# Two transposes of a hybrid attention trunk move from TensorE to VectorE and to the stores

## The chip, the cores and the metric

The kernel runs on one core of a Trainium2 chip. The metric is device time in microseconds for one launch. The core has five engines, each with an instruction queue of its own that is worked in order: TensorE (PE: matrix products, and transposes as products with an identity), VectorE (DVE), ScalarE (ACT), GpSimd (POOL) and SyncE (SP), which here does nothing but issue DMAs. Sixteen DMA engines carry the transfers that SP and ACT issue.

## The reference

One layer of a hybrid trunk over 2048 latent tokens behind 256 context tokens, width 1024. One projection of the normalized input feeds two token mixers; the one that matters here is a gated DeltaNet with four heads of 128, run forward and backward over chunks of 64 tokens. Cut to what the change touches:

```python
def _gdn_inputs(qkv_raw, ...):
    qkv = silu(_short_conv(qkv_raw, conv_w))          # 5 taps along the tokens
    q, k, v = split(qkv)                              # 4 heads of 128 each
    q, k = _l2norm(q) * 128 ** -0.5, _l2norm(k)

def _gdn_chunked(q, k, v, g, beta, s0, ...):          # for each direction
    gc = cumsum(g)                                    # within a chunk of 64 tokens
    decay = where(incl, exp(gc[:, None] - gc[None, :]), 0)
    a_mat = where(strict, (kb @ kc.T) * decay, 0)     # the keys' decayed Gram matrix
    t_mat = triangular_solve(a_mat, eye)              # its inverse, unit lower triangular
    u, w = t_mat @ (vc * bc), t_mat @ (kb * exp(gc))
    ...                                               # scan over the chunks with u, w, q, k
```

Everything is float32 in and out; the large products are split into high and low float32r parts.

## The kernel before

Eighteen blocks of 128 tokens (two of context, sixteen of latent) are worked in this order. First come the input norms, the transposed input `hh`/`hl` and the attention keys. Then `qkv(ORDER)` runs over the column blocks m of the projection: the four value heads m = 8 to 11, then the four key heads m = 4 to 7, and after them the four query heads m = 0 to 3 together with the attention queries. For each m there are five segments (256 tokens of context, four times 512 latent tokens): `fm_dense` on PE gives `lps` with channels on the partitions, ScalarE copies it to `y`, `conv` makes `cacc` (four passes on VectorE at L625, one more at L627 with ScalarE's tanh ahead of it), and `finish` does what the head needs. So there are twenty calls of `finish` for the value heads and twenty for the key heads, each on nn = 2 or 4 blocks.

For a value head, `finish` needs the tokens on the partitions: PE transposes each 128x128 block of `cacc` into the PSUM tile `zt` (L657), ScalarE copies it to `st` (L675), and one DMA stores it to `vsp` (L648).

For a key head, `finish` also stores `cacc` itself (`kTsp`, L654), makes the transposed keys the same way (`ksp`), and forms the Gram matrix of each block: `gps` on PE (L666), times the decay tile `dtl`, which is loaded from `Dsp` (L632) into a single buffer, gives `p` on VectorE (L668). `p` serves the backward direction. Its transpose serves the forward direction: PE transposes (L680) into the same two PSUM buffers as `gps`, ScalarE copies to `pt` (L682). Of each of the two, `spill_blocks` stores the two 64x64 diagonal squares to `Nsp` (L639, two DMAs) and one 64x64 off-diagonal square to `offsp` (L640, one DMA). `p` and `pt` share the tag `o` of two buffers.

Later, `base` loads the planes of `Nsp` with one 64x64 square on each partition (L796) and inverts them on VectorE, beside the gate projections (`rest_run`) on PE; `base4` does the same for the last four blocks (L839), and the scan loads `vsp`, `ksp` and `offsp`.

The order of each engine's instructions is fixed when the program is built: a planner simulates the program and lays every queue out in the order of its simulated times. In the run an engine waits at the head of its queue for the semaphores that the instruction names. Nothing behind it passes.

Of the kernel before, what the change touches and what calls it, by code (L numbers as in the profile page):

```python
# [7 lines left out]
F32 = mybir.dt.float32  # L8
# [11 lines left out]
NC = NB + NCB  # L20
H = 4
# [19 lines left out]
def _hybrid(ctx, tc, nc, V, S, G, T, ins, out, dbg, upto):  # L41
    dma = nc.sync.dma_start
# [5 lines left out]
    def dscr(name, shape, dt=F32):  # L48
        return dram.tile(shape, dt, name=name)
# [10 lines left out]
    ident = cst.tile([128, 128], F32, name="ident")  # L60
# [21 lines left out]
    g = pers.tile([128, NC, 8], F32, name="g")  # L82
# [9 lines left out]
    ksp = dscr("ksp", [NC, 128, H, 128])  # L92
    vsp = dscr("vsp", [NC, 128, H, 128])
    Dsp = dscr("Dsp", [NC, 128, H, 128])

    Nsp = [dscr(f"Nsp{d}", [NC, H, 2, 64, 64]) for d in range(2)]
    offsp = [dscr(f"offsp{d}", [NC, 64, H, 64]) for d in range(2)]
    QDsp = dscr("QDsp", [NB, 128, H, 128])
    brT = dscr("brT", [NC, 8, 128])
# [43 lines left out]
    def psum(tag, shape, dt=F32, name=None):  # L143
        _, p, banks = pst["left" if tag in pst["left"][2] else "right"]
        return p.tile(shape, dt, name=name or tag, tag=tag, bufs=banks[tag])
# [104 lines left out]
    if True:  # L250
# [283 lines left out]
        for gi in range(8):  # L534
# [10 lines left out]
            o = gi % 2 * 256  # L545
# [89 lines left out]
    def spill_blocks(d, t, c0, nn, h):  # L635

        for b in range(2):
            r = slice(b * 64, b * 64 + 64)
            dma(Nsp[d][c0:c0 + nn, h, b].rearrange("c r i -> r c i"), t[r, :, r])  # L639
        dma(offsp[d][c0:c0 + nn, :, h].rearrange("c r i -> r c i"), t[64:128, :, 0:64])  # L640

    def finish(m, z, c0, n):

        h = m % 4
        nn = n // 128
        b0 = c0 - NCB
        zc = [z[:, j * 128:(j + 1) * 128] for j in range(nn)]
        spill = lambda dst, t: dma(dst.rearrange("c p d -> p c d"), t)  # L648
        if m < 4:
            dma(qTsp[h, :, b0 * 128:b0 * 128 + n], z)  # L650
            kT = pb.tile([128, 4, 128], F32, name="kTl", tag="st")
            dma(kT, kTsp[h, :, c0 * 128:c0 * 128 + n].rearrange("p (c t) -> p c t", t=128))
        elif m < 8:
            dma(kTsp[h, :, c0 * 128:c0 * 128 + n], z)  # L654
        ps = psum("zt", [128, 4, 128])
        for j in range(nn):
            T.transpose(ps[:, j], zc[j], ident)  # L657
        if m < 8:
            dt = decay_of(h, c0, nn)
            for j in range(nn):  # L660
                junk = pb.tile([128, 128], BF16, name="junk", bufs=1)
                dst = ssk[:, c0 + j, h:h + 1] if m >= 4 else alpha[:, b0 + j, h:h + 1]
                S.activation(junk, ps[:, j], AF.Square, accum_out=dst)
            gps = psum("gps", [128, 4, 128])
            for j in range(nn):
                T.matmul(gps[:, j], lhsT=zc[j] if m >= 4 else kT[:, j], rhs=zc[j], start=True, stop=True)  # L666
            p = pb.tile([128, 4, 128], F32, name="p", tag="o")[:, :nn]
            V.tensor_tensor(p, gps[:, :nn], dt, op=ALU.mult)  # L668
            if m >= 4:
                spill_blocks(1, p, c0, nn, h)  # L670
            else:
                spill(QDsp[b0:b0 + nn][:, :, h], p)
        if m >= 4:
            st = pb.tile([128, 4, 128], F32, name="st")[:, :nn]
            S.copy(st, ps[:, :nn])  # L675
            spill((ksp if m < 8 else vsp)[c0:c0 + nn, :, h], st)
        if 4 <= m < 8:
            pps = psum("gps", [128, 4, 128])
            for j in range(nn):
                T.transpose(pps[:, j], p[:, j], ident)  # L680
            pt = pb.tile([128, 4, 128], F32, name="pt", tag="o")[:, :nn]
            S.copy(pt, pps[:, :nn])  # L682
            spill_blocks(0, pt, c0, nn, h)

    def qkv(order, after, w=None, beside=()):
        w = w or weights(w_in[:, order[0] * 128:order[0] * 128 + 128], KT)
# [95 lines left out]
    def base(si, npool, pool, fr, bk):  # L782


        n = 8 * len(fr)
        h1 = max(32, n)
        N = npool.tile([128, 64, 64], F32, name="N")
        nb = npool.tile([128, 64], F32, name="nb")
        if n < h1:
            G.memset(N[0:h1], 0.0)  # L790
            G.memset(nb[0:h1], 0.0)
        for d, chunks in ((0, fr), (1, bk)):
            for i0, c, k in runs(chunks):
                p0 = d * h1 + i0 * 8
                dma(nb[p0:p0 + 8 * k], brT[c:c + k, d * 4:d * 4 + 4].rearrange("c h (b t) -> c (h b) t", b=2))
                dma(N[p0:p0 + 8 * k], Nsp[d][c:c + k].rearrange("c h b r i -> (c h b) r i"))  # L796
        for q in range(4):
            r, w = slice(q * 16, q * 16 + 16), q * 16 + 16
            V.tensor_tensor(N[0:h1, r, 0:w], N[0:h1, r, 0:w],
                            nb[0:h1, 0:w].unsqueeze(1).to_broadcast([h1, 16, w]), op=ALU.mult)  # L800
            V.tensor_tensor(N[h1:h1 + n, r, 0:w], N[h1:h1 + n, r, 0:w],
                            nb[h1:h1 + n, r].unsqueeze(2).to_broadcast([n, 16, w]), op=ALU.mult)
        yield 9
        A = N[0:h1 + n]
        for m in range(1, 63):
            tmp = pool.tile([128, 1376], F32, name="btmp")
            r = 63 - m
            tv = tmp[0:h1 + n, :r * m].rearrange("p (r j) -> p r j", j=m)
            V.tensor_tensor(tv, A[:, m + 1:, m].unsqueeze(2).to_broadcast([h1 + n, r, m]),  # L809
                            A[:, m, 0:m].unsqueeze(1).to_broadcast([h1 + n, r, m]), op=ALU.mult)  # L810
            V.tensor_tensor(A[:, m + 1:, 0:m], A[:, m + 1:, 0:m], tv, op=ALU.add)  # L811
            yield 2 * (65 + 1.04 * r * m) / 1e3

        for q in range(4):
            r, w = slice(q * 16, q * 16 + 16), 64 - q * 16
            G.affine_select(A[:, r, q * 16:], A[:, r, q * 16:], pattern=[[1, 16], [-1, w]], base=0,
                            channel_multiplier=0, compare_op=ALU.is_gt, fill=0.0)
        V.memset(A.rearrange("p r c -> p (r c)")[:, ::65], 1.0)
        for d, chunks in ((0, fr), (1, bk)):
            p0 = d * h1  # L820
            dma(Xset[d][si].rearrange("c h b r j -> (c h b) (r j)"), N[p0:p0 + n].rearrange("p r j -> p (r j)"))
            for ci, c in enumerate(chunks):
                Xsp[d][c] = Xset[d][si][ci]
        yield 1

    def base4(fr, bk):


        N = bs2.tile([128, 64, 64], F32, name="N")
        nb = bs2.tile([128, 64], F32, name="nb")  # L830
        buf = bs2.tile([128, 1376], F32, name="btmp")
        X = buf[:, 0:1024].rearrange("p (r s) -> p r s", s=16)
        tmp, nc_ = buf[:, 1024:1312], buf[0:32, 1312:1376]
        G.memset(nb[0:32], 1.0)
        G.memset(nc_, 1.0)
        for d, chunks in ((0, fr), (1, bk)):
            c, p0 = chunks[0], d * 16
            dma((nc_, nb)[d][p0:p0 + 16], brT[c:c + 2, d * 4:d * 4 + 4].rearrange("c h (b t) -> c (h b) t", b=2))
            dma(N[p0:p0 + 16], Nsp[d][c:c + 2].rearrange("c h b r i -> (c h b) r i"))  # L839
        G.memset(X, 0.0)  # L840
        for q in range(4):
            G.memset(X[q * 32:q * 32 + 32].rearrange("p r s -> p (r s)")[:, 16 * q:16 * q + 976:65], 1.0)
        yield
        for q in range(4):
            r, w = slice(q * 16, q * 16 + 16), q * 16 + 16
            V.tensor_tensor(N[0:32, r, 0:w], N[0:32, r, 0:w], nc_[:, 0:w].unsqueeze(1).to_broadcast([32, 16, w]), op=ALU.mult)
            V.tensor_tensor(N[0:32, r, 0:w], N[0:32, r, 0:w], nb[0:32, r].unsqueeze(2).to_broadcast([32, 16, w]), op=ALU.mult)
        for q in range(1, 4):
            dma(N[q * 32:q * 32 + 32], N[0:32])
        yield  # L850
        for m in range(63):
            r, n = 63 - m, m // 4 + 1
            tv = tmp[:, :r * n].rearrange("p (r s) -> p r s", s=n)
            V.tensor_tensor(tv, N[:, m + 1:, m].unsqueeze(2).to_broadcast([128, r, n]),
                            X[:, m, 0:n].unsqueeze(1).to_broadcast([128, r, n]), op=ALU.mult)
            V.tensor_tensor(X[:, m + 1:, 0:n], X[:, m + 1:, 0:n], tv, op=ALU.add)
            if m % 6 == 5:
                yield
        for d, chunks in ((0, fr), (1, bk)):
            for ci, c in enumerate(chunks):  # L860
                for q in range(4):
                    p0 = q * 32 + d * 16 + ci * 8
                    dma(X4sp[d, ci, q], X[p0:p0 + 8])
        yield
# [817 lines left out]
```

## Time and profile before

| | us |
|---|---|
| median of three runs | 1965.65 |
| lowest and highest run | 1961.01, 1967.35 |
| the profiled execution | 1973.82 |
| its span, first to last instruction | 1972.1 |

The span is what the profile's rows add up to; the 1.7 us between it and the execution's time lie outside the instructions. The profiled execution is 8.2 us above the median of the runs. The stages that the change touches are the value heads from about 150 to 290 us and the key heads from about 290 to 440 us; the query heads follow to about 630 us, then the gates with `base`, the scan from about 900, attention from about 1320, and the output projections to the end. In a row of the timeline the first number is the start and the second the duration, both in us; in brackets stands the idle time ahead of it and what ended it. `SPq` marks an instruction of SP's sequencer: its duration is the time that issuing the DMA held SP, not the transfer's.

### The profile page before, as it was taken

The page shows a single profiled execution, that of the slowest core. Times are in us where ns is not written, and L with a number is a line of the kernel's source. Part 1 is how long each engine was busy: PE and PEld are TensorE (multiplying, and loading weights), DVE is VectorE, ACT ScalarE, POOL GpSimd, SP SyncE. Part 2 cuts the span into 40 slices and gives each one's busy share as a digit, 9 for nine tenths or more (in the row PEclk, how much of TensorE's full clock was granted, in tenths as well). Part 3 has the DMA queues.
Part 4 walks back from the last instruction along what each step waited for, and adds up shares of the span by engine and source line. Part 5 has one row for each costly group of instructions (what it writes and reads, how often), then busy time and mean ns, then how long its engine had stood idle before and what let it go on. Part 6 is the DMA issues. An engine that isn't in the chain of part 4 may idle for free. (4 is left out here: it accounts for less than half of the span.)

```text
span 1972.1 us, 32045 instructions
## 1 busy us (share of the span) xinstructions
PE 1910.1 (97%) x10943; PEld 1606.0 (81%) x10943; DVE 1477.4 (75%) x2853; ACT 815.9 (41%) x2008; POOL 657.4 (33%) x750
## 2 busy tenths in 40 slices
PE   6899999989999999999999999999999999999999
PEld 3888888778998787887888888888878887878787
DVE  7889766677776999999778767544787777757864
ACT  6865545554444322211122233324675555532321
POOL 2652111235543201104222334422555444430353
PEclk9999999999999999999999999999999999999999
DMA  7553226765546633537887777755555555448362
GB/s 267 162 154 94 86 89 160 188 163 168 155 149 162 188 106 115 152 93 211 226 243 224 225 217 228 205 157 183 173 164 168 172 164 171 137 120 283 123 224 86
DMA packets 385463, 333.12 MB, mean 169 GB/s; under 512 B 83800, under 2 KB 307344, under 8 KB 384660
## 3 DMA queue, kind: packets, MB, share of 16 engines
q1 hardware_dynamic: 366292, 295.40, 51.7%
q10 hardware_dynamic: 19008, 35.67, 4.9%
q8 instruction: 87, 1.43, 0.3%
q14 instruction: 76, 0.62, 0.1%
HBM read 220.28 MB, written 109.13 MB: 167 GB/s over the span
## 5 line engine op out<-in xcount | busy, mean ns | idle before, releaser
L586 PE MATMUL rps<-hh,wh 128*128 128x512 f32 x768 | 309.8, 403 | 4.3 <-DVE rt L880 3.2
L587 PE MATMUL rps<-hl,wh 128*128 128x512 f32 x768 | 308.3, 401 | 0.0
L588 PE MATMUL rps<-hh,wl 128*128 128x512 f32 x768 | 307.2, 400 | 0.0
L625 DVE SCALAR_TENSOR_TENSOR cacc<-y,cw,cacc 128x512 f32<-128x512 f32 (+1 forms) x224 | 165.0, 758 | 21.1 <-ACT cacc L623 18.8
L586 PEld LDWEIGHTS rps<-hh,wh 128*128 128x128 f32 x768 | 145.4, 189 | 39.8 <-DVE rt L880 3.7
L588 PE MATMUL lps<-hh,wl 128*128 128x512 f32 (+1 forms) x448 | 171.7, 383 | 1.2 <-DVE wl L244 1.2
L586 PE MATMUL lps<-hh,wh 128*128 128x512 f32 (+1 forms) x448 | 172.0, 384 | 0.8 <-POOL wh L243 0.6
L588 PEld LDWEIGHTS rps<-hh,wl 128*128 128x128 f32 x768 | 145.3, 189 | 32.7
L587 PEld LDWEIGHTS rps<-hl,wh 128*128 128x128 f32 x768 | 145.7, 190 | 31.8
L587 PE MATMUL lps<-hl,wh 128*128 128x512 f32 (+1 forms) x448 | 171.0, 382 | 0.0
L1006 DVE TENSOR_TENSOR pl<-pt,ph 128x512 fp32r<-128x512 f32 x156 | 105.5, 685 | 45.8 <-ACT ph L1004 44.9
L1004 ACT CAST ph<-pt 128x512 fp32r<-128x512 f32 x156 | 90.6, 585 | 110.7 <-PE pt L1002 72.1
L878 ACT ACTIVATE rt<-rps 128x512 f32<-128x512 f32 x96 | 57.2, 596 | 185.1 <-PE rps L588 168.2
L978 DVE CUSTOM_DVE_ANT_0 pr<-sc,band,sk 128x640 f32<-128x640 f32 (+1 forms) x128 | 106.7, 862 | 19.9 <-PE sc L974 12.7
L811 DVE TENSOR_TENSOR N<-N,btmp 128x62 f32<-128x62 f32 (+30 forms) x124 | 118.1, 953 | 3.0
L988 POOL TENSOR_SCALAR pr<-pr,sm 128x640 f32<-128x640 f32 (+1 forms) x128 | 101.0, 809 | 55.8 <-DVE sm L986 40.3
L809 DVE TENSOR_TENSOR btmp<-N 128x62 f32<-128x62 f32 (+30 forms) x124 | 115.8, 934 | 3.1
L980 ACT ACTIVATE pr<-pr,sm 128x640 f32<-128x640 f32 (+1 forms) x128 | 104.0, 815 | 24.6 <-DVE sm L978 20.9
L244 DVE TENSOR_TENSOR wl<-wr,wh 128x512 fp32r<-128x512 f32 x120 | 90.8, 768 | 24.1 <-POOL wh L243 21.2
L1293 PE MATMUL pps<-yh,wph 128*128 128x512 f32 x256 | 105.7, 415 | 2.1 <-DVE tb L1304 2.0
L243 POOL TENSOR_SCALAR wh<-wr 128x512 fp32r<-128x512 f32 x72 | 50.3, 711 | 159.4 <-PE lps L587 57.2
L1295 PE MATMUL pps<-yh,wpl 128*128 128x512 f32 x256 | 101.9, 399 | 1.2 <-POOL wpl L1255 1.2
(396 smaller groups left out, 4961.4 us busy)
## 6 DMA issues: line engine op xcount, KB each, us to landing
wr<-in_w_in_dram SPq DMA_DIRECT2D x120, 256.0 KB
kw<-Ksp SPq DMA_DIRECT2D x28, 384.0 KB
x<-vsp SPq DMA_DIRECT2D x36, 256.0 KB
k<-ksp SPq DMA_DIRECT2D x34, 256.0 KB
kT<-kTsp SPq DMA_DIRECT2D x34, 256.0 KB
wm<-in_w_mod_dram SPq DMA_DIRECT2D x16, 512.0 KB
xt<-in_x_dram SPq DMA_DIRECT2D x16, 512.0 KB
dtl<-Dsp SPq DMA_DIRECT2D x32, 256.0 KB
```

Of the source, the lines that this page charges most:

```text
L586: T.matmul(ps, lhsT=wh[:, k], rhs=xh[:, k], start=k == 0, stop=False)
L587: T.matmul(ps, lhsT=wh[:, k], rhs=xl[:, k], start=False, stop=False)
L588: T.matmul(ps, lhsT=wl[:, k], rhs=xh[:, k], start=False, stop=k == kt - 1)
L625: V.scalar_tensor_tensor(a, y[:, t:t + n], cw[:, m, t:t + 1], a, op0=ALU.mult, op1=ALU.add)
L809: V.tensor_tensor(tv, A[:, m + 1:, m].unsqueeze(2).to_broadcast([h1 + n, r, m]), A[:, m, 0:m].unsqueeze(1).to_broadcast([h1 + n, r, m]), o ...
L811: V.tensor_tensor(A[:, m + 1:, 0:m], A[:, m + 1:, 0:m], tv, op=ALU.add)
L978: V.tensor_tensor_reduce(s_, ps[:, o:768], band[:, b0:b0 + W + 256], -0.125, sk[:, 1, hd:hd + 1], ALU.add, ALU.min, sm[:, h, 1:2])
L980: S.activation(s_, s_, AF.Exp, scale=-1.0, bias=sm[:, h, 1:2], accum_out=sm[:, h, 2:3])
L988: G.tensor_scalar(p[:, h, :W + 256], p[:, h, :W + 256], sm[:, h, 3:4], 1.0, op0=ALU.mult, op1=ALU.mult)
L1006: V.tensor_tensor(pl, pt, f32(ph), op=ALU.subtract)
L1293: T.matmul(ps, lhsT=wh[:, k, ms], rhs=hs[k], start=k == 0, stop=False)
L1295: T.matmul(ps, lhsT=wl[:, k, ms], rhs=hs[k], start=False, stop=k == 3)
```

## The change

VectorE transposes 32x32 squares inside a tile, each square in its place. The change lets it turn `cacc` of the value heads that way, and `p` of the key heads, and leaves it to the DMA that stores the result to put each square where it belongs. The PE transposes of both and the ScalarE copies out of PSUM go. The keys' own transposes for `ksp` stay on PE, since ScalarE takes their squares' sums from PSUM.

A turned square has its 32 rows on 32 partitions, so a store takes 32 partitions. One store of `vsp` (128 partitions, runs of 128 numbers) becomes four (32 partitions, runs of 32 numbers). The three stores of `pt` (64 partitions, runs of 64) become six (32 partitions, runs of 32). The planes of `Nsp` for the forward direction get a new order in DRAM, head first, so that in a store the block and the half of the square make one step; `base` and `base4` read them with the head inside the block again, by `blocks_of`. The bytes stay the same.

```diff
-    Nsp = [dscr(f"Nsp{d}", [NC, H, 2, 64, 64]) for d in range(2)]
+    Nsp = [dscr("Nsp0", [H, 2, NC, 64, 64]), dscr("Nsp1", [NC, H, 2, 64, 64])]
...
+    def spill_turned(t, c0, nn, h):
+        for g in range(4):
+            r, b = slice(g * 32, g * 32 + 32), g // 2
+            q = slice(g % 2 * 32, g % 2 * 32 + 32)
+            dma(Nsp[0][h, b, c0:c0 + nn].rearrange("c (k a) i -> a (c k) i", a=32)[:, :, q],
+                t[r, b, :2 * nn])
+            if g < 2:
+                dma(offsp[0][c0:c0 + nn, :, h].rearrange("c (k a) i -> a (c k) i", a=32)[:, :, q],
+                    t[r, 1, :2 * nn])
+
+    def blocks_of(d, c, k):
+        if d:
+            return Nsp[1][c:c + k].rearrange("c h b r i -> (c h b) r i")
+        return Nsp[0][:, :, c:c + k].rearrange("h b c r i -> c (h b) (r i)")
...
+        if m >= 8:
+            st = pb.tile([128, 4, 128], F32, name="st")[:, :nn]
+            V.transpose(st, z.rearrange("p (c t) -> p c t", t=128))
+            for g in range(4):
+                dma(vsp[c0:c0 + nn, :, h, g * 32:g * 32 + 32].rearrange("c (k a) d -> a (c k) d", a=32),
+                    st[g * 32:g * 32 + 32].rearrange("a c (k d) -> a (c k) d", d=32))
+            return
...
-            spill((ksp if m < 8 else vsp)[c0:c0 + nn, :, h], st)
+            spill(ksp[c0:c0 + nn, :, h], st)
         if 4 <= m < 8:
-            pps = psum("gps", [128, 4, 128])
-            for j in range(nn):
-                T.transpose(pps[:, j], p[:, j], ident)
-            pt = pb.tile([128, 4, 128], F32, name="pt", tag="o")[:, :nn]
-            S.copy(pt, pps[:, :nn])
-            spill_blocks(0, pt, c0, nn, h)
+            pt = pb.tile([128, 2, 8, 32], F32, name="pt", tag="o")
+            V.transpose(pt[:, :, :2 * nn].rearrange("p b (c k) i -> p c b (k i)", k=2),
+                        p.rearrange("p c (b i) -> p c b i", b=2))
+            spill_turned(pt, c0, nn, h)
```

The planner lays the queues out anew. In the middle of the key heads SP's queue reads like this before (`Nsp_88` and `offsp_90` are the backward direction's, stored from `p`; `Nsp_87` and `offsp_89` the forward direction's, stored from `pt`):

```order
L654 DMA kTsp<-cacc 128x512
L632 DMA dtl<-Dsp 128x4x128
L654 DMA kTsp<-cacc 128x512
L639 DMA Nsp_87<-pt 64x4x64 x2
L640 DMA offsp_89<-pt 64x4x64
L639 DMA Nsp_88<-p 64x4x64 x2
L640 DMA offsp_90<-p 64x4x64
L648 DMA ksp<-st 128x4x128
L632 DMA dtl<-Dsp 128x4x128
```

Between the load of `dtl` and the next one stand the stores of the earlier finish's `pt`, then those of this finish's `p`. After the change the same stretch of SP's queue is (lines have moved by 8 to 24):

```order
L632 DMA dtl<-Dsp 128x4x128
L665 DMA ksp<-st 128x4x128
L671 DMA kTsp<-cacc 128x512 x2
L639 DMA Nsp_88<-p 64x4x64 x2
L640 DMA offsp_90<-p 64x4x64
L647 DMA Nsp_87<-pt 32x8x32
L650 DMA offsp_89<-pt 32x8x32
L647 DMA Nsp_87<-pt 32x8x32
L650 DMA offsp_89<-pt 32x8x32
L647 DMA Nsp_87<-pt 32x8x32 x2
L632 DMA dtl<-Dsp 128x4x128
```

Now the stores of `p` and of `pt` of the same finish stand together, nine in a row, and the next load of `dtl` behind them; `ksp` and `kTsp` have moved to the place behind the load.

VectorE's queue in the same stage, before:

```order
L668 TENSOR_TENSOR p<-gps,dtl 128x512
L700 COPY y<-y 128x2
L625 SCALAR_TENSOR_TENSOR cacc<-y,cw,cacc 128x256
L701 COPY y<-y 128x2
L625 SCALAR_TENSOR_TENSOR cacc<-y,cw,cacc 128x256 x3
```

And after:

```order
L692 TENSOR_TENSOR p<-gps,dtl 128x512
L625 SCALAR_TENSOR_TENSOR cacc<-y,cw,cacc 128x512
L720 MEMSET y 128x2
L703 STREAM_TRANSPOSE pt<-p 128x4x2x64
L627 SCALAR_TENSOR_TENSOR cacc<-y,cacc 128x512
```

The transpose of `p` stands one or two instructions behind the product that makes it, where before VectorE went on with the convolution.

More of the change, by code (lines that the diff above doesn't have):

```diff
@@ L795, in base @@
                 dma(nb[p0:p0 + 8 * k], brT[c:c + k, d * 4:d * 4 + 4].rearrange("c h (b t) -> c (h b) t", b=2))
-                dma(N[p0:p0 + 8 * k], Nsp[d][c:c + k].rearrange("c h b r i -> (c h b) r i"))
+                dma(N[p0:p0 + 8 * k] if d else N[p0:p0 + 8 * k].rearrange("p r i -> p (r i)"), blocks_of(d, c, k))
         for q in range(4):
@@ L838, in base4 @@
             dma((nc_, nb)[d][p0:p0 + 16], brT[c:c + 2, d * 4:d * 4 + 4].rearrange("c h (b t) -> c (h b) t", b=2))
-            dma(N[p0:p0 + 16], Nsp[d][c:c + 2].rearrange("c h b r i -> (c h b) r i"))
+            dma(N[p0:p0 + 16] if d else N[p0:p0 + 16].rearrange("p r i -> p (r i)"), blocks_of(d, c, 2))
         G.memset(X, 0.0)
```

## The prediction

> **What bounds the kernel now.** I read the page first, then the busy time by stage, then who waits in the stage that the change touches, then that stage's instructions in order of time. The page's first part:
>
> ```profile
> PE 1910.1 (97%) x10943; PEld 1606.0 (81%) x10943; DVE 1477.4 (75%) x2853; ACT 815.9 (41%) x2008; POOL 657.4 (33%) x750
> ```
>
> TensorE is busy nearly all the time, so an instruction that leaves PE shortens the run wherever nothing else holds the stage. The change lies in two stages: the value heads (m = 8 to 11, about 150 to 290 us) and the key heads (m = 4 to 7, about 290 to 440 us). Busy time by stage (x is a count; the last three columns are granted clock, DMA share and GB/s):
>
> ```profile
> 150.00:290.00 140.00, 140.00 (x698) 116.35 (x697) 111.47 (x195) 76.18 (x173) 28.88 (x28) 1.00 0.30 92
> 290.00:440.00 150.00, 141.50 (x854) 120.96 (x853) 100.28 (x203) 78.28 (x258) 31.64 (x31) 1.00 0.65 165
> 440.00:630.00 190.00, 188.56 (x1293) 171.12 (x1293) 141.00 (x326) 86.05 (x265) 90.61 (x105) 1.00 0.52 158
> ```
>
> The value stage is full on PE (140 of 140) with VectorE third at 111.47. The key stage is not full: 8.5 us of PE are idle though 150 us pass. The waits there (us in total, times, longest) say what sets its pace:
>
> ```profile
> DVE p L668 <- DMA dtl<-Dsp: 23.0, 15, 2.6
> PE gps L680 <- DVE p L668: 2.5, 4, 0.7
> PE gps L680 <- DVE y L698: 2.1, 1, 2.1
> ```
>
> In 15 of 20 finishes VectorE's product p waits for the decay tile dtl. That tile has one buffer, and its load stands in SP's queue behind stores. One turn of it, SP's queue and then VectorE:
>
> ```profile
> 332.98 0.60 SPq L632 DMA_DIRECT2D dtl<-Dsp  x1
> 334.32 1.23 SPq L639 DMA_DIRECT2D Nsp<-pt  x2
> 335.59 0.60 SPq L640 DMA_DIRECT2D offsp<-pt  x1
> 336.86 1.23 SPq L639 DMA_DIRECT2D Nsp<-p  x2
> 338.14 0.61 SPq L640 DMA_DIRECT2D offsp<-p  x1
> 338.85 0.55 SPq L648 DMA_DIRECT2D ksp<-st  x1
> 339.44 0.53 SPq L654 DMA_DIRECT2D kTsp<-cacc  x1
> 340.01 0.45 SPq L632 DMA_DIRECT2D dtl<-Dsp  x1
> ```
>
> ```profile
> 336.14 0.69 DVE L668 TENSOR_TENSOR p<-gps,dtl 128x512 f32<-128x512 f32 x1 [2.50 <-DMA dtl<-Dsp]
> ```
>
> Read it as a closed loop. From the issue of dtl (332.98) to p (336.14) pass 3.16 us. From p's start to the end of its three stores (338.75) pass 2.61. The stores of ksp and kTsp take 1.16 with their gaps, and the next dtl goes out at 340.01: 7.03 us. The three stores of pt, the transposed copy, fall inside the 3.16 us in which dtl is on its way and cost nothing. The second and the last of the stage's twenty loads:
>
> ```profile
> 296.55 0.47 SPq L632 DMA_DIRECT2D dtl<-Dsp  x1
> ...
> 429.24 0.55 SPq L632 DMA_DIRECT2D dtl<-Dsp  x1
> ```
>
> Eighteen turns in 132.69 us are 7.37 us each. PE has at most 141.50/20 = 7.1 us of work in a turn, so loop and PE are now about level.
>
> **Value heads.** Seventy-two PE transposes and twenty ScalarE copies go. What a transpose takes of PE is read from starts, since ends overlap:
>
> ```profile
> 425.11 0.40 PE L588 MATMUL lps<-hh,wl 128*128 128x512 f32 x1
> 425.34 0.60 PE L657 MATMUL zt<-ident,cacc 128*128 128x128 f32 x4
> 425.70 0.48 PE L586 MATMUL lps<-hh,wh 128*128 128x512 f32 x1
> 426.01 0.40 PE L587 MATMUL lps<-hl,wh 128*128 128x512 f32 x1
> ```
>
> A 512-wide matmul follows the one before after 0.23 us. Four transposes and one matmul take 425.34 to 426.01, 0.67 us, so four cost 0.44 and one 0.11. 72 x 0.11 = 7.9 us off a stage that PE fills. The twenty copies lie on ScalarE, busy 76.18 of 140, and are worth nothing by themselves.
>
> VectorE gets twenty transposes: sixteen of 512 elements a partition, four of 256. The trace has no transpose on VectorE. The nearest rows:
>
> ```profile
> L305 DVE TENSOR_SCALAR xt<-xt,rstd x18: 470/486/953, 32.0 to 112.2; 128x512 f32<-128x512 f32 x18
> L668 DVE TENSOR_TENSOR p<-gps,dtl 128x512 f32<-128x512 f32 (+1 forms) x20 | 12.7, 637 | 25.9 <-DMA dtl<-Dsp 23.0 <-DMA kTsp<-cacc 1.7 <-PE zt L657 1.2
> L345 DVE TENSOR_TENSOR wml<-wm,wmh 128x1024 fp32r<-128x1024 f32 x15 | 17.6, 1219 | 5.1 <-PE mps L313 2.7 <-ACT wmh L344 2.4
> ```
>
> A 512-wide pass takes 0.49 us at least; 1.22, a pass twice as long, is the bound if each element needs two. I take p's time, since p has the same shapes and the same twenty calls: 12.7 us. VectorE then has 111.5 + 12.7 = 124 us of work against PE's 132. It still fits, but at 94% in-order waits begin to show, so I count 6 of the 7.9 us; all 7.9 is one end, and 0 the other, where each transpose takes 1.22 (111.5 + 18 x 1.22 = 133, no room left). The Trainium skill, page VectorE: DVE Perf Modes, section The three transpose paths, gives 311 ns for 128x128 in bf16 on VectorE against 390 ns on TensorE and calls VectorE the fastest for 32x32 squares. Four of its 311 would be an estimate of 1.24 us for 512 columns, VectorE would be as full as PE and the stage's gain near 0; and the rows above have TensorE at 0.11 us a transpose in steady flow, not 0.39.
>
> SP's stores of vsp become 80 instead of 20. SP issues little there (wr loads and these), and nothing that is due stands behind them, so they cost nothing; if they stalled, ScalarE's gm, which shares the buffers of st, would be late next.
>
> **Key heads.** PE loses 72 transposes of p (L680), 7.9 us, and the 4.6 us of waits for VectorE shown above. None of it counts if the loop sets the pace, and the loop gets longer. pt now follows p on VectorE after one conv pass (its row in this stage, mean in ns after the busy time):
>
> ```profile
> L625 DVE SCALAR_TENSOR_TENSOR cacc<-y,cw,cacc 128x512 f32<-128x512 f32 (+1 forms) x81 | 58.3, 720 | 4.5 <-ACT cacc L623 3.0
> ```
>
> It is ready 0.69 + 0.72 + 0.69 = 2.1 us after p's start, earlier than the 2.6 us at which p's own stores are out. So its stores, six in place of three, now stand directly behind p's, and the next dtl behind all nine (the order of SP's queue in the section on the change). They leave the shade of dtl's flight and enter the loop; ksp and kTsp, 1.16 us, take their place in the shade. The new turn is 3.16 + 2.61 + 0.1 of gap + 6c = 5.9 + 6c, where c is the time from one such store to the next.
>
> No store from 32 partitions of SBUF to DRAM is in the trace. Nearest issues (ns, least/median/most):
>
> ```profile
> L639 SPq DMA_DIRECT2D Nsp<-pt x40: 574/592/1747, 299.1 to 436.6; - x40
> L648 SPq DMA_DIRECT2D vsp<-st x20: 359/360/458, 154.5 to 283.9; - x20
> L849 SPq DMA_DIRECT2D N<-N x3: 568/592/598, 983.5 to 989.2; - x3
> L839 SPq DMA_DIRECT2D N<-Nsp x2: 312/366/420, 967.2 to 968.2; - x2
> L863 SPq DMA_DIRECT2D X4sp<-btmp x16: 263/291/1018, 1209.8 to 1249.3; - x16
> ```
>
> They have 64, 128, 32 (SBUF on both sides), 16 and 8 partitions. With the 0.05 us between neighbours c lies between 0.34 (8 partitions) and 0.64 (64). In the loop above stores of 128 partitions that follow others take 0.53 to 0.55 rather than 0.36, so I lean to the upper half: c = 0.55. A turn is then 9.2 us, and 19 turns cost 19 x (9.2 - 7.37) = 35 us. Ends: c = 0.34 gives 7.95 and +11; c = 0.64 gives 9.75 and +45.
>
> **Smaller pieces.** The planes of Nsp for direction 0 are laid out head first, so their load has eight pieces outermost, not 64 rows, and may use fewer DMA engines. VectorE takes this half first and then waits for the other direction anyway:
>
> ```profile
> 633.02 3.02 DVE L799 TENSOR_TENSOR N<-N,nb 64x256 f32<-64x256 f32 x4 [5.74 <-DMA N<-Nsp]
> 642.13 3.04 DVE L801 TENSOR_TENSOR N<-N,nb 64x256 f32<-64x256 f32 x4 [4.29 <-DMA N<-Nsp]
> ```
>
> Up to 4.3 us of delay are covered by that second wait; beyond it PE's gate matmuls go on and the scan starts only when they are done. I cost it 0.
>
> **Sum.** -6 (value heads) + 35 (key heads) = +29 us on the profiled execution's 1973.8, that is 2003 for it. That execution is 8 us above the median of the three runs, 1965.65, and the forecast is against the median: 1995 us. The stage after (188.56 of 190 on PE) has no slack that gives any back. With both ends: -8 + 11 = +3 and 0 + 45 = +45, 1969 to 2011.
>
> **Rivals.**
> Faster, because PE runs ahead. If PE could work on the next heads and on the q heads while the stores catch up, the loop would end in the shade of the q stage, and the run would win 2 x 7.9 of transposes and 4.6 of waits, 20 us: 1945. For it: PE idles only 8.5 us in a stage whose product waited 23. Against: PE takes its instructions in order, gps (two PSUM buffers) stands between the head matmuls and its buffer comes free with the p of two finishes before. It decides if PE can be 35/9.2, about four, finishes ahead; two is what the buffers give.
> Cheap stores. If c is near the 0.34 of 8 partitions the turn is 7.95, and +11 - 8 leaves +3: 1969, within the noise, and at 0.42 (16 partitions: 0.37 and the 0.05) 8.4, +20 - 8, 1978.
> Small packets. The stores write 128-byte runs. In the value stage now 0.30 of 16 engines move 92 GB/s, which is 27 ns for each 512 bytes. If a 128-byte run took twice that, one store of 256 runs would hold 16 engines 0.85 us, longer than its issue; six would take 5.1 us, the turn 11.0 and the stage +69: 2029. The Trainium skill, DMA: Bandwidth & Descriptors, Specifications, puts line rate at 512 bytes and above and says that smaller ones are read, modified and written back; by it this rival would hold. No row here shows a 128-byte run's time alone.
>
> **How the numbers follow.** Forecast 0.68; cheap stores 0.15, half of it within 0.3% and half slower; PE ahead 0.10; small packets 0.07. About 0.3% (6 us) is what the spread of the runs, 1961.01 to 1967.35, lets a measurement tell from no change. Slower: 0.68 + 0.08 + 0.07 = 0.83; same 0.07; faster 0.10. The forecast's own range is 1981 (c = 0.45, all 7.9 won: 19 x 1.23 = 23 - 8) to 2011. For eight in ten I leave out the case below and the case above and take the cheap stores in: 1966 to 2014.
>
> **What would show it.** Right: twenty dtl loads at 9 us or so apart (8 to 9.8), six stores between p's and dtl at about 0.55 each, PE idle some 45 us more between the first and last p, VectorE waiting for dtl in nearly every finish; the value stage shorter by 5 to 8 us, transposes near 0.69. Wrong: dtl turns of 7.4 or less, or PE full in the key stage; transposes over 1 us with PE waiting for VectorE in the value stage; or a load of N that lands after the second half.

## The result and the profile after

The changed kernel takes 1998.71 us (median of five runs, 1994.15 to 2004.48) against 1965.65 (1961.01 to 1970.12): a ratio of 1.0162, 95% interval 1.0143 to 1.018, 33 us slower. Its profiled execution took 1999.75 us, its span is 1998.0. The page's first part, and the two stages that the change touches (columns as in the prediction):

```profile
PE 1902.2 (95%) x10799; PEld 1597.0 (80%) x10799; DVE 1499.2 (75%) x2893; ACT 797.1 (40%) x1968; POOL 661.9 (33%) x750
```

```profile
150.00:290.00 140.00, 134.84 (x638) 111.24 (x637) 129.36 (x234) 71.60 (x173) 32.80 (x28) 0.99 0.42 95
290.00:440.00 150.00, 132.69 (x723) 111.88 (x722) 94.34 (x189) 62.16 (x209) 29.59 (x29) 0.96 0.59 148
```

PE lost its 144 transposes, yet it waits in both stages: 5.2 us in the first, which it filled before, and 17.3 in the second, against 8.5. VectorE is at 129 of 140 in the first. In both the granted clock (0.99, 0.96) is no longer 1.00.

VectorE's transposes, by line (mean ns of one after the busy time, then its idle time ahead of them):

```profile
L674 DVE STREAM_TRANSPOSE st<-cacc 128x512 f32<-128x512 f32 (+1 forms) x20 | 13.0, 652 | 7.2 <-DMA vsp<-st 7.2
L703 DVE STREAM_TRANSPOSE pt<-p 128x512 f32<-128x512 f32 (+1 forms) x20 | 13.0, 652 | 0.0
```

Ahead of the transposes of the value heads VectorE stands idle 7.2 us, until an earlier store of `vsp` has freed the buffer `st`.

One turn of the key heads' loop, SP's queue and then VectorE:

```profile
352.34 0.45 SPq L632 DMA_DIRECT2D dtl<-Dsp  x1
...
356.44 1.25 SPq L639 DMA_DIRECT2D Nsp<-p  x2
357.73 0.61 SPq L640 DMA_DIRECT2D offsp<-p  x1
358.44 0.55 SPq L647 DMA_DIRECT2D Nsp<-pt  x1
359.03 0.46 SPq L650 DMA_DIRECT2D offsp<-pt  x1
359.53 0.46 SPq L647 DMA_DIRECT2D Nsp<-pt  x1
360.03 0.45 SPq L650 DMA_DIRECT2D offsp<-pt  x1
360.52 0.94 SPq L647 DMA_DIRECT2D Nsp<-pt  x2
361.51 0.45 SPq L632 DMA_DIRECT2D dtl<-Dsp  x1
```

```profile
355.72 0.69 DVE L692 TENSOR_TENSOR p<-gps,dtl 128x512 f32<-128x512 f32 x1 [5.62 <-DMA dtl<-Dsp]
```

From the load (352.34) to p 3.38 us; the three stores of p end at 358.34; then the six of pt take 358.44 to 361.51, 3.07 us or 0.51 each; then the next load. This turn is 9.17. The second and the last of the twenty loads:

```profile
287.66 0.43 SPq L632 DMA_DIRECT2D dtl<-Dsp  x1
...
454.34 1.77 SPq L632 DMA_DIRECT2D dtl<-Dsp  x1
```

Eighteen turns in 166.68 us are 9.26 us each, where they were 7.37. From the first p of the key heads to the last (281.6 to 458.8 us after, 293.4 to 432.4 before) pass 38 us more. How much of that reaches the end is seen at the last p of the query heads, the last start in these rows (all 36 products of key and query heads; before, then after):

```profile
L668 DVE TENSOR_TENSOR p<-gps,dtl x36: 423/691/692, 293.4 to 626.6; 128x512 f32<-128x512 f32 x32, 128x256 f32<-128x256 f32 x4
```

```profile
L692 DVE TENSOR_TENSOR p<-gps,dtl x36: 417/692/694, 281.6 to 642.1; 128x512 f32<-128x512 f32 x32, 128x256 f32<-128x256 f32 x4
```

The key heads begin 12 us earlier, lose 38, and the query heads give 11 back: +15.5 us at 642. The rest of the 33 comes later. Busy time between the first and the last key-head p, before and after:

```profile
293.00:433.00 140.00, 131.54 (x782) 111.88 (x781) 92.23 (x177) 73.62 (x244) 27.25 (x29) 1.00 0.66 167
```

```profile
281.00:459.00 178.00, 159.96 (x896) 136.84 (x895) 117.81 (x242) 73.78 (x248) 39.45 (x41) 0.95 0.57 142
```

PE idles 18.0 us in the longer stretch, 8.5 in the shorter: only 9.5 more. The other 28 us PE was at work: on products of the q pass (the attention queries), which start in this stage in both kernels (394 us), and at a clock of 0.95.

Then the load of N. VectorE's first products of the two large bases' forward half:

```profile
653.68 3.02 DVE L821 TENSOR_TENSOR N<-N,nb 64x256 f32<-64x256 f32 x4 [10.93 <-DMA N<-Nsp]
675.03 3.03 DVE L821 TENSOR_TENSOR N<-N,nb 64x256 f32<-64x256 f32 x4 [5.29 <-DMA N<-Nsp]
```

The loads and the store behind them, and the first of the loads in the kernel before:

```profile
640.63 0.61 SPq L818 DMA_DIRECT2D N<-Nsp  x1
...
660.72 0.59 SPq L818 DMA_DIRECT2D N<-Nsp  x1
661.97 0.51 SPq L818 DMA_DIRECT2D N<-Nsp  x1
663.86 0.33 SPq L903 DMA_DIRECT2D zasp<-rt  x1
```

```profile
625.01 0.52 SPq L796 DMA_DIRECT2D N<-Nsp  x1
```

The first load is used 13.05 us after its issue; before it was 8.0 (625.01 to 633.02). And PE stands still. The waits of this stretch after the change (us in total, times, longest):

```profile
ACT rt L900 <- DMA zasp<-rt: 15.0, 1, 15.0
PE rps L586 <- DVE rt L902: 10.0, 2, 8.7
```

```profile
683.56 0.69 DVE L902 SCALAR_TENSOR_TENSOR rt<-rt,rps 128x512 f32<-128x512 f32 x1
```

Read from the store up: the store of a gate product `rt`, issued at 663.86 behind two loads of 1 MB, lands 17 us later (12 before); its buffer is one of two; ScalarE's next `rt` waits 15.0 us for it, until 681.07; VectorE's `rt` comes at 683.56, behind ScalarE's and behind the N products of the other direction, which VectorE works from 680.49 to 683.53; and PE waits for the PSUM bank that this `rt` frees. Before, ScalarE's wait was 8.9 us and PE's 3.2.

### The profile page after: what moved, and what is told of

It is laid out like the page before. It is cut to its first block, busy times and chain, and to the rows that moved or that the text cites. A ratio compares the mean times of both kernels' runs of the same rounds, so it can differ in the third digit from the quotient of the medians.

```text
span 1998.0 us, 31889 instructions
## 1 busy us (share of the span) xinstructions
PE 1902.2 (95%) x10799; PEld 1597.0 (80%) x10799; DVE 1499.2 (75%) x2893; ACT 797.1 (40%) x1968; POOL 661.9 (33%) x750
## 5 line engine op out<-in xcount | busy, mean ns | idle before, releaser
L586 PE MATMUL rps<-hh,wh 128*128 128x512 f32 x768 | 309.4, 403 | 11.1 <-DVE rt L902 10.0
L586 PEld LDWEIGHTS lps<-hh,wh 128*128 128x128 f32 x448 | 86.3, 193 | 20.6 <-DVE xn L449 2.1
```

What stands on the lines that cost most here:

```text
L586: T.matmul(ps, lhsT=wh[:, k], rhs=xh[:, k], start=k == 0, stop=False)
```

## The experiments

All times stand against runs of the kernel before on the same chip (medians 1966.1 to 1968.4), as ratios with 95% intervals; 0.1% is 2 us.

**Each part alone.** Values: the kernel before with only this.

```diff
+        if m >= 8:
+            V.transpose(st, z.rearrange("p (c t) -> p c t", t=128))
+            ...                               # four stores, return
```

> Only the value heads are turned by VectorE; the key heads' transposes, stores and the N load stay as they were. Theory (the loss sits in the key heads' loop, the value part is a gain): last value store some 7 us and first key-head product some 12 us earlier than before, dtl loads still about 7.4 us apart, time 1952 to 1960 against 1965.65. Rival 1 (the value part gains nothing, because the key heads' loop or the q stage takes it back): 1963 to 1968. Rival 2 (VectorE is made too full and the value part itself costs): over 1969.

1970.81 us, ratio 1.0021 (1.001 to 1.0032): not the gain expected, but slightly slower, in the second rival's range. Its key heads do start at 280.7 us instead of 293.4, but its last p of the query heads comes when it came before:

```profile
L675 DVE TENSOR_TENSOR p<-gps,dtl x36: 417/691/692, 280.7 to 626.0; 128x512 f32<-128x512 f32 x32, 128x256 f32<-128x256 f32 x4
```

In the value stage PE now waits for VectorE's share of the decays, which before it never did between 129 and 290 us, and a half-clock window follows (the wait in total, then one 20 us stretch of that kernel):

```profile
PE dps L204 <- DVE gm L202: 3.3, 2, 1.7
```

```profile
210.00:230.00 20.00, 18.26 (x84) 15.12 (x83) 19.55 (x37) 11.72 (x29) 5.24 (x5) 0.91 0.34 76
```

VectorE is busy 19.55 of 20 us here. It also waits 6.1 us between 150 and 270 us for `vsp` stores that free `st`; how much of PE's wait comes from these and how much from the added transposes, no run separates.

Keys: the changed kernel, with the values as before.

```diff
-        if m >= 8:
-            ...
-            spill(ksp[c0:c0 + nn, :, h], st)
+            spill((ksp if m < 8 else vsp)[c0:c0 + nn, :, h], st)
```

> Only the key heads' decayed Gram matrix is turned by VectorE (with its six stores and Nsp0's new layout and load); the values go by PE transposes as before. Theory (six stores ahead of the one dtl buffer's next load): dtl loads 9.1 to 9.4 us apart against 7.37, key stage +34 to +40, of which the q stage gives back about 11, the N load adds 5 to 8: time 1993 to 2005. Rival (the loss comes from both parts together, VectorE too full): 1970 to 1985.

2003.34 us, 1.0187 (1.0169 to 1.0205): the theory's range. The turns are 8.99 us, just under the 9.1 to 9.4 expected; the last p of the query heads comes at 649.2, 22.6 us late. So the loss lies in the key heads' part, which here includes the load of N. Beside them the values' part is worth some 5 us (2003.34 against 1998.71, though the intervals overlap a little): of the 12 to 13 us by which it lets the key heads start earlier, 7 are left at the last p of the query heads here (642.1 against 649.2), and none where the loop is short (626.0 against 626.6).

**Six stores instead of three,** from PE's transposes, the rest as before.

```diff
-            spill_blocks(0, pt, c0, nn, h)
+            for g in range(4):                # 32 partitions each, rows of 64
+                dma(Nsp[0][c0:c0 + nn, h, b, x]..., pt[r, :, b * 64:b * 64 + 64])
+                if g >= 2:
+                    dma(offsp[0][c0:c0 + nn, x, h]..., pt[r, :, 0:64])
```

> The kernel before, with the three stores of the turned Gram matrix split into six of 32 partitions with rows of 256 B (same bytes, same place in DRAM; transposes still by PE, N load as before). Theory (what costs is the time SP takes to issue six stores ahead of the dtl load, not the squares' small packets): six take about 3 us where three took 1.7, so turns of 8.6 to 9.3 us and a time of 1985 to 1998. Rival (packets of 128 B in the squares' layout, or VectorE's transposes, are the cost): turns of 7.4 us and 1963 to 1970.

1977.56 us, 1.0054 (1.0039 to 1.0069), turns of 8.06 us: less than the theory expected, more than its rival. SP's queue there says why:

```profile
348.78 0.60 SPq L632 DMA_DIRECT2D dtl<-Dsp  x1
...
351.23 1.30 SPq L686 DMA_DIRECT2D Nsp<-pt  x3
...
354.07 1.25 SPq L639 DMA_DIRECT2D Nsp<-p  x2
...
356.24 1.34 SPq L686 DMA_DIRECT2D Nsp<-pt  x3
...
359.05 0.43 SPq L632 DMA_DIRECT2D dtl<-Dsp  x1
```

A turned copy that comes by way of PE and ScalarE is ready later, so most of its stores are issued while the next dtl is on its way (351.23); only in some turns do they stand ahead of it (356.24). So their number costs something (8.06 against 7.37 us a turn), and their place costs more (9.26).

**N's new layout alone:** the kernel before with `Nsp0` head first and `blocks_of` in the loads; stores as they were.

> The kernel before, with only the first direction's buffer in DRAM laid out head first, so that the base's load of N has the changed kernel's source (stores stay three of 64 partitions). Theory (the load's shape makes it land later, VectorE's next operations and through them PE wait): loads of 13 us instead of 8 us, PE's wait for rt about 9 us instead of 3.2, time 1970 to 1975. Rival (the longer load in the changed kernel came from what ran beside it, or is hidden): 1964 to 1968.

1979.54 us, 1.0067 (1.0053 to 1.0081): 13 us, more than the theory's 1970 to 1975 allowed. The prediction had costed this part of the change at nothing.

```profile
624.74 0.61 SPq L803 DMA_DIRECT2D N<-Nsp  x1
```

```profile
638.06 3.02 DVE L806 TENSOR_TENSOR N<-N,nb 64x256 f32<-64x256 f32 x4 [11.15 <-DMA N<-Nsp]
```

```profile
650.00:670.00 20.00, 11.09 (x47) 8.64 (x46) 12.37 (x20) 5.87 (x10) 3.64 (x3) 0.82 0.77 165
```

13.3 us from issue to use, with nothing else changed, and PE busy 11.1 of the 20 us behind it (16.8 before). The Trainium skill, DMA: Bandwidth & Descriptors, section Why a DMA increments its semaphore by 16 and not by 1, says that a DMA is spread over the largest number up to 16 that divides the slowest dimension of both sides; here that dimension of the source went from 64 to 8. The longer landing agrees; the engines in use show in no row here.

**Opening the loop.** First by place: pt's stores held back until the next dtl load is issued.

```diff
             dt = decay_of(h, c0, nn)
+            while late:
+                spill_turned(*late.pop())
...
-            spill_turned(pt, c0, nn, h)
+            late.append((pt, c0, nn, h))
```

> The changed kernel, with pt's six stores put behind the next piece's dtl load instead of ahead of it (everything else as in the changed kernel, the squares' 128 B rows and VectorE's transposes too). Theory (the key heads' turn is long because the six stores, ready 0.7 us after p, stand ahead of the one dtl buffer's next load on SP): turns of 6.9 to 7.6 us against 9.26, key stage some 33 us shorter, and with what the q stage gives back 15 to 25 off the changed kernel: 1974 to 1984; the N load's 13 us stay. Rival (the squares' small packets or VectorE's share set the turn): turns over 8.5 us and 1993 to 2002.

Then by a second dtl buffer in the decays' pool, in the changed kernel, in the kernel before and in the one with the values alone:

```diff
-        dt = pb.tile([128, 4, 128], F32, name="dtl", bufs=1)[:, :nn]
+        turn[0] += key
+        dt = (dc.tile([128, 4, 128], F32, name="dtk", bufs=1) if key and turn[0] % 2 else
+              pb.tile([128, 4, 128], F32, name="dtl", bufs=1))[:, :nn]
```

> The changed kernel, with a second buffer for the key heads' dtl load, so that the load no longer waits for p to be read. Theory (the one buffer closes the loop): PE sets the turn, 6.8 to 7.4 us, time 1972 to 1984 as with the stores put behind. Rival (SP's queue itself is full, or the clock's half-speed windows and not the loop are the loss): 1990 to 2000.

> The kernel before, with the second dtl buffer alone. If the loop of 7.37 us per turn bound before's key stage too, PE's waits there (about 9 us from 340 to 500 us) go: 1956 to 1962. If PE's own work bound it (100% busy in most of that stage): 1963 to 1968, no change.

> The kernel with only the values turned by VectorE, with the second dtl buffer. Theory (PE's 7.9 us of value transposes are removed, but the value heads lose 4 to 5 us of it where PE waits for VectorE's gm, and two half-clock windows follow): with the key heads' loop open the first part is kept: 1957 to 1965. Rival (the q stage's own work ends at the same time whatever comes ahead): 1966 to 1971 as without the buffer.

All four missed the theory's time: 2013.64 (1.0226, 1.0201 to 1.0252), 2009.73 (1.0211, 1.0187 to 1.0235), 1977.99 (1.0053, 1.0037 to 1.0069) and 1972.74 (1.002, 1.0004 to 1.0035). The turn did as expected in the first (7.51 us), and there the last key-head p came at 422.8 us instead of 458.8. But the q pass, whose products had filled PE's waits, moved. Its first products, in the changed kernel, with the stores held back, and with the second buffer:

```profile
L413 PE MATMUL tmps<-qwh,hh x256: 276/281/542, 393.6 to 630.9; 128*128 128x256 f32 x128
```

```profile
L413 PE MATMUL tmps<-qwh,hh x256: 276/281/353, 439.1 to 645.2; 128*128 128x256 f32 x128
```

```profile
L413 PE MATMUL tmps<-qwh,hh x256: 276/281/561, 426.1 to 640.5; 128*128 128x256 f32 x128
```

With the stores held back the planner put the q pass's weight loads behind the last key heads (431.7 us instead of 363.1). With the second buffer GpSimd makes these weights at 423.5 us instead of 367.2, behind its work for the key heads' norms. In the kernel before with a second buffer the products move as well, from 394.0 to 412.5 us: the buffer stands in memory that the q pass's weights take over, and GpSimd's first write of them waits 22.0 us for a p of the key heads. So these three runs changed two things at once and settle nothing about the loop's price. They agree with PE's waits in the key heads being cheap only as long as other work is at hand: with the stores held back PE waits 23.1 us there for the convolution's `cacc`. In the fourth the q pass stayed (398.8 us, 399.9 without the buffer) and the key heads ended 17 us earlier (402.2 us instead of 419.4), yet the last p of the query heads came at 625.9, as without the buffer: there the rival held. The next run opens the loop and keeps that work in place:

```diff
+        dt = (ev.tile([128, 4, 128], F32, name="dtk", tag="rt", bufs=2) if key else ...)
...
+            with tc.high_priority(1500) if hv == 0 else nullcontext():
                 ...                           # the q pass's weight loads
+                with tc.high_priority(800) if hv == 0 and c < NCB + 8 else nullcontext():
                     q_block(pool, c, hv, tm_dense(c, wh, wl, 256), wn)
```

> The changed kernel with two buffers for the key heads' dtl load (in ev's two rt buffers, idle in that stage, so that no memory of the q pass is held), and with the q pass's first weight loads and first four products given a higher priority, so that they stay where the changed kernel has them (loads at the 11th to 12th dtl load, first tmps at the 14th piece). It is the run with two buffers again, without what went wrong there (tmps began at 426 us instead of 394). Theory (the six stores ahead of the one buffer's load cost net about 19 us, loop 38 less what the q stage gives back): turns of 7 to 7.6 us, 1975 to 1987. Rival (the key heads' loop costs nothing net, since PE always has q work to fill it with; the loss is the N load, VectorE's value part and half-clock windows): 1995 to 2005.

1984.44 us, 1.0086 (1.0064 to 1.0107): the theory's range, 14 us off the changed kernel. The products p of the key heads, then those of the query heads:

```profile
L693 DVE TENSOR_TENSOR p<-gps,dtk x20: 414/688/693, 283.8 to 432.2; 128x512 f32<-128x512 f32 x16, 128x256 f32<-128x256 f32 x4
L693 DVE TENSOR_TENSOR p<-gps,dtl x16: 676/681/693, 454.3 to 626.6; 128x512 f32<-128x512 f32 x16
```

The key heads end at 432.2 us instead of 458.8, and the query heads at 626.6, as before the change. The finishes were 7.8 us apart, not 7 to 7.6. What stays, 0.86% or 17 us, is as much as N's layout (13) and the values (4) cost alone. One thing was left open: the priority also lets the q pass begin 9 us earlier than in the changed kernel (384.8 against 393.6), and no run has it without the second buffer, so not all of the 14 us is shown to be the loop's.

**N's wait.** The products of N with `nb` in the two large bases, the first that use the load, are put behind later `rt` products on VectorE, in the changed kernel (fourth and eighth) and in the one before (third and sixth; the edit of the changed kernel):

```diff
+            with tc.issue_after(rts[(3, 7)[si]].ins):
                 V.tensor_tensor(N[0:h1, r, 0:w], ...)
                 V.tensor_tensor(N[h1:h1 + n, r, 0:w], ...)
```

> The changed kernel, with the first products of N in the two large bases put behind rt number 4 and 8 on VectorE, so that VectorE doesn't stand waiting for the load; the load itself stays as slow. Theory (13 us of the loss come from the load because VectorE waits for it and holds rt, and PE behind rt; two of the three places are mended here): PE's wait of 8.7 us for rt gone, no half-clock window at 680 us, 8 to 12 off: 1987 to 1992. Rival (the base's chain is what the stage waits for, so that a later start is paid elsewhere): 1997 to 2002.

> The kernel before, with the same products of N put behind rt number 3 and 6. Theory: PE's wait of 3.2 us for rt and the two half-clock windows behind it (660.7 us, 6.8 us long, 3.4 us lost) go: 5 to 7 off, 1960 to 1963 against 1966 to 1968. Rival (the base's chain is the path): 1966 to 1970.

Both theories failed: 2010.94 us (1.0219, 1.0198 to 1.0241) and 1994.54 (1.0145, 1.0119 to 1.0171), 12 and 26 us worse than without the edit, and worse than the rivals had it. VectorE's standing at N was not what held PE: with it gone in the changed kernel PE still waits for `rt`:

```profile
PE rps L586 <- DVE rt L905: 11.1, 3, 7.9
```

And what starts late in a base ends late. The bases' stores of their results (first and last start), in the kernel before and with the products held back in it:

```profile
L821 SPq DMA_DIRECT2D Xsp<-N x4: 507/550/767, 804.8 to 954.9; - x4
```

```profile
L822 SPq DMA_DIRECT2D Xsp<-N x4: 512/547/584, 812.9 to 969.4; - x4
```

The products end 3 us later at the first base and 15 at the second (648.5 and 675.7 us against 645.2 and 660.8), the stores come 8 and 14.5 us later, and the attention's first load of queries is issued at 1353.0 us instead of 1335.3; the rest of the 26 us was not traced. With N's new layout alone the same stores come 6 us late and that load 12 us (1347.2), nearly the 13 us that the layout costs.

**VectorE's room in the value heads.** The values alone, with one of VectorE's two decay products a chunk moved to GpSimd:

```diff
-                    (G, V, V)[n].tensor_tensor(gm, ...
+                    (G, V, G)[n].tensor_tensor(gm, ...
```

> The kernel with only the values turned by VectorE, and with one of VectorE's two gm products of each chunk's decay moved to GpSimd, which takes 18 products of 0.68 us off VectorE between 150 and 265 us. Theory (VectorE is what the value heads lack: PE waited 4.6 us for gm there, and a half-clock window of 1.7 us followed, out of 7.9 us of transposes that PE no longer does): PE's waits for gm under 1 us, no half-clock window before the key heads, first key-head product 2 to 5 us earlier than the 280.7 us of the run with the values alone. If the lead lasts to the end: 1959 to 1964. Rival (the q stage ends at 616 us whatever lead comes into it, as in the four runs that so far reached it early): 1965 to 1971. Second rival (GpSimd's products are late in their turn, 1.07 to 1.6 us each): PE waits for gm 5 us or more and 1970 to 1976.

1974.0 us, 1.0032 (1.0017 to 1.0046): the second rival's size, by another way. The product left on VectorE is late, not GpSimd's:

```profile
PE dps L204 <- DVE gm L202: 6.6, 4, 2.7
```

The convolution's passes on VectorE (150 to 270 us), with the values alone and here:

```profile
L625 DVE SCALAR_TENSOR_TENSOR cacc<-y,cw,cacc 128x512 f32<-128x512 f32 (+1 forms) x75 | 58.1, 786 | 1.4 <-ACT cacc L623 0.8
```

```profile
L625 DVE SCALAR_TENSOR_TENSOR cacc<-y,cw,cacc 128x512 f32<-128x512 f32 (+1 forms) x70 | 61.9, 889 | 2.4 <-ACT cacc L623 1.4
```

They take 889 ns in place of 786 while GpSimd has 36 decay products in place of 18. The 512-wide passes alone go from 832 to 963 ns. The work moved off VectorE came back as slower work; that GpSimd's products beside it are the reason is argued from this one pair of runs, not shown. None of the twelve beats the kernel before; the best use of the change that was found is not to make it.

## Why the prediction was right, and where it was not

The forecast (1995, +29 us) and the result (1998.71, +33) agree. The mechanism named, six stores on SP ahead of the one dtl buffer's next load, is shown: turns of 9.26 us, 7.51 with the same stores behind the load, and with the loop opened and the q pass kept in place the delay at the query heads' end is gone. But three terms of the sum were off, and they cancelled, so that the number came this close is in part luck.

- The turn, 5.9 + 6c: right. 3.38 us from load to p where 3.16 was put, c = 0.51 where 0.55 was put, and 9.26 us where 9.2 was forecast. Short issues of about 0.30 us, which the rival of cheap stores needs, appear only where a store stands alone; in a row they take 0.41 to 0.55. One reading behind the 7.37 us of the kernel before was drawn from a single turn: that pt's three stores cost nothing there. In eight of its eighteen turns they reach past p and hold p's stores back (in the shown turn those follow p after 0.72 us, in these after 1.1 to 2.4), and in two more they stand ahead of the next load (404.35 and 420.99 us).
- What the turn costs: the step "the stage after has no slack that gives any back" failed. The loop cost 38 us in its own stage. At the last query-head p 22.6 are left with the keys alone, and 15.5 in the whole change, where the values' lead is counted in; the run with the loop opened agrees with the 15.5 (1.0162 against 1.0086), with what it leaves open. PE idled 9.5 us more, not 45. The rival in which PE runs ahead held in part: not on the next heads, where PE waits for p to free one of the two PSUM buffers (`gps` behind p, 9.8 us from 290 to 440), but on the q pass.
- N's load, costed 0: it is 13 us. The step that failed is "PE's gate matmuls go on". They wait for a PSUM bank that is freed behind a store behind the load and behind the N products, and the base that starts later ends later, with the scan behind it. The text named a load that lands after the second half as what would make it wrong, and had no price for it.
- Value heads, -6: alone they are +4, within the change about -5. The transposes cost what p cost (652 ns mean, forecast 637, and 0.70 us for 512 columns; not the estimate of 1.24 us that the forecast had worked out from the Trainium skill, VectorE: DVE Perf Modes, The three transpose paths), and VectorE fitted by its sum (129.4 of 140, forecast 124). By its order it did not: PE waits 4.0 us for decay products, where it waited for none, and with the values alone the clock falls behind such a wait (0.91). The stores of `vsp` were put at nothing too, and VectorE waits 7.2 us for them.
- Small packets: not seen. From dtl's load to p pass 3.3 us (median) where 3.2 passed before, the rest of the turn is mostly SP's issue time, and with the same stores behind the load the turn is 7.51 us.

By parts, then: keys alone +37 (loop some 23, N 13), values beside them -5, together +32. In the forecast: +35, -6.

The step that was missing altogether is the clock. The same kernel in slices of 3.4 us:

```profile
673.40:676.80 3.40, 2.22 (x10) 1.47 (x8) 1.76 (x3) 0.00 (x0) 0.00 (x0) 1.00 1.17 139
676.80:680.20 3.40, 0.00 (x0) 0.00 (x0) 1.63 (x3) 0.00 (x0) 0.00 (x0) 0.99 0.75 158
680.20:683.60 3.40, 0.00 (x0) 0.00 (x0) 3.08 (x5) 2.40 (x4) 0.96 (x1) 0.50 0.50 166
683.60:687.00 3.40, 2.69 (x6) 2.17 (x7) 3.37 (x4) 1.37 (x3) 2.57 (x3) 0.50 0.28 82
687.00:690.40 3.40, 3.40 (x9) 2.67 (x8) 3.37 (x6) 1.83 (x3) 1.52 (x2) 0.50 0.71 189
690.40:693.80 3.40, 3.40 (x16) 2.73 (x15) 3.30 (x5) 0.19 (x1) 1.40 (x1) 1.00 0.97 309
```

Behind a slice in which PE mostly waits, the clock column falls to 0.50 and comes back a slice after PE is busy again: 9 matmuls in place of 16. The Trainium skill, TensorE: Matmul & The Clock Gate, section What's actually happening, gives this as a gate that watches PE in windows of 3413 ns; the rows agree, the stretch at 0.50 being three of these long (680.2 to 690.4). Over the runs the mean clock is 0.985 against 0.994 before, by estimate at most 20 us of the 33 (0.01 of 1998); in the two profiled executions it is 0.986 against 0.991, at most 10 of the 26 us between them. It is no further term beside the parts above; it is how a wait of a few us can cost more than its length, and it hides in the terms as each was measured. How much of the loss would stay at full clock no run separates.

Open also: in five kernels (before, N's layout alone, the values with one and with two buffers, the loop opened) the last head matmul starts at 608.7 to 608.9 us, though their key heads end between 402 and 432. That every lead of these is taken back by then is shown; what holds that time was not found.

## What to carry to other kernels

A copy that is ready sooner is not free: in an in-order queue its stores may move from the shade of a load to a place ahead of it, so look at what each store now stands in front of, and ask whether the engine that waits has other work at hand before you price the wait. Price a load whose layout changed by its own duration and follow everything that travels behind it, stores that free buffers above all. When an experiment opens a loop, check that the rest of the queue stayed where it was.

## What was not expected of the hardware

- In the key heads a store from 32 partitions holds SP 0.30 us where it stands alone (442.81 us) and 0.41 to 0.46 in a row, the first of a row mostly 0.55; from 64 partitions it is 0.57 to 0.61. Half the partitions cost three quarters.
- VectorE turns 128x512 float32 in 32x32 squares in 0.70 us, as long as a 512-wide product of two tensors (0.69).
- A load of the same 1 MB took 13 us instead of 8 to its use with 8 pieces outermost instead of 64, and the small store issued 2 us behind such loads landed 17 us after its issue instead of 12.
- The clock's falls differ from run to run: the profiled execution of the kernel before had a mean of 0.991, its other runs mostly 0.993 to 0.996. That is not all of the 8 us by which it stood above the median: four more runs at 0.991 took 1965.3 to 1971.2 us.
